# Expert weights of a mixture-of-experts layer in 2 MB blocks instead of 1 MB blocks

## The chip, the cores and the metric

The kernel runs on one core of one Trainium2 chip. The metric is the device time of one execution in microseconds (us). Three runs of the kernel before took 1173.51, 1174.28 and 1174.98 us, so their median is 1174.28 us. One further execution was taken by the profiler; all rows below come from it.

## The reference

One decoder layer on 256 tokens of width 1024, all in float32. Two attention branches work on one input projection, are gated, added and projected, and a layer norm gives `h`. Then 32 experts follow, of which each token uses four:

```
logits = h @ w_router + b_router
top_vals, top_idx = top_k(logits, 4);  gates = softmax(top_vals)
for each expert e:
    a   = h @ w_up[e] + b_up[e]                 # 1024 x 2048
    g   = min(a[:, :1024], 7);  lin = clip(a[:, 1024:], -7, 7)
    y   = ((lin + 1) * g * sigmoid(1.702 * g)) @ w_down[e] + b_down[e]   # 1024 x 1024
    acc = acc + combine[:, e] * y
out = layer_norm(2**0.25 * h + acc)
```

The weights of one expert are 8 MB (`w_up`) and 4 MB (`w_down`); all 32 are 384 MB (a MB of weights is 1,048,576 bytes here, and GB/s are decimal), and every one is read once from HBM.

## The kernel before, in words

**Stages.** First come projections and attention, with packed weights `w_pre` of 1 MB a block. Then the output stage (line 641 on) builds the two branches' mix and its projection, in eight steps `j`. Each step splits weight blocks into a high and a low part with `part`, on ScalarE and VectorE, into one of three scratch tiles: `sh`, `sy` and `sacc`. `sacc` lies in the place that the tile `acc` has later. Then the router chooses experts, and the expert stage works on pairs of experts `ea`, `ea + 1`: `gather` multiplies `h` by a selection matrix `pm` so that each expert's tokens (at most 64) stand in columns, `up_products` runs over eight row blocks `k` of `w_up`, `swiglu` and `transpose_y` follow, `down_products` runs over four blocks `a` of `w_down`, and `add_scattered` adds the pair's rows to `acc`. The last two pairs (28 and 30) are written out by hand: up of both, then down of both.

**Weight blocks.** `up_view` and `down_view` cut an expert into blocks of 128 partitions by 2048 numbers: 1 MB, 8 KB in each partition, contiguous in HBM. They land in tiles of the pools `ring1` (7), `ring2` (5), `ring3` (4), `ring4` (2) and `ringx` (2). `ring1` and `ring2` also carry the last `w_pre` blocks: a ring tile is free for an expert block as soon as its own `w_pre` block has been split. Twenty expert blocks (`ahead`) and two more, which land in `acc` and in `moe`'s tile `wy`, can be fetched before the first product.

**What sets the order.** All loads are issued by SyncE (SP, one queue). PE, VectorE and ScalarE follow the written order in the expert stage (`manual_schedule`); the order on SP is set by the framework's planner for the whole program. SP works strictly in order: a load that waits holds back every load behind it. Each load waits until its place is free, and eight completion semaphores are used in turn, so that a load also waits for the landing of the load eight places earlier.

The names that matter below: `acc`, `ahead`, `slot` (before) and `slot2` (after), `fetch_up`, `fetch_down`, `bias_parts` (line 564: loads `b_up` and `b_down` rows into the one tile `braw`, which GpSimd then works on), `columns`, and the hand-written last pairs.

Of the kernel before, what the change touches and what calls it, by code (L numbers as in the profile page):

```python
# [10 lines left out]
F32 = mybir.dt.float32  # L11
# [19 lines left out]
NR1, NR2, NR3, NR4, NRX, NSP = 7, 5, 4, 2, 2, 3  # L31
# [26 lines left out]
def decoder_layer(ctx: ExitStack, tc: tile.TileContext, A, dbg=None):  # L58
# [4 lines left out]
    ring1 = ctx.enter_context(tc.tile_pool(name="ring1", bufs=NR1))  # L63
# [15 lines left out]
    def slot(dtype=F32):  # L79

        if once:
            return once.pop()
        turn[0] += 1
        pool = seq[(turn[0] - 1) % len(seq)]
        return pool.tile([P, 2048], dtype, name="w", tag="x" if pool.name == "ringx" else "w")
# [457 lines left out]
    ring2 = ctx.enter_context(tc.tile_pool(name="ring2", bufs=NR2, reuse_waits="tile", side="right"))  # L543
    ringx = ctx.enter_context(tc.tile_pool(name="ringx", bufs=NRX, reuse_waits="tile", side="right"))
# [13 lines left out]
    ve.tensor_scalar(brd, ident[:NE, :NE], br, None, op0=OP.mult)  # L558
    wr = per.tile([P, KD, NE], F32, name="wr")
# [76 lines left out]
    ring4 = ctx.enter_context(tc.tile_pool(name="ring4", bufs=NR4, reuse_waits="tile", side="right"))  # L636
# [4 lines left out]
    for j in range(KD):  # L641
        if j % 2 == 0:
            wo = load(15 + 3 * (j // 2), 2)
        ps = misc().rearrange("p (a t) -> p a t", a=2)
        w = part(wo, j % 2, KD)
        for a, o in enumerate((oa, ob)):
            for k in range(4):
                mm3(ps[:, a], (w[0][:, 4 * a + k], w[1][:, 4 * a + k]), (o[0][:, k], o[1][:, k]),
                    k == 0, k == 3)
        t = held["g", j][1]  # L650
        ve.tensor_mul(t, ps, t)
        ve.tensor_add(t[:, 0], t[:, 0], t[:, 1])
        if j:
            w = part(wu, (j - 1) % 2, 1)
            for b in range(NT):
                w_out(j - 1, b, w)
        if j % 2 == 0:
            wu = load(27 + j // 2, 2)
        if j == 3:
            xr = ringx.tile([P, NT, D], F32, name="xr", tag="x")  # L660
# [11 lines left out]
    ring3 = ctx.enter_context(tc.tile_pool(name="ring3", bufs=NR3, reuse_waits="tile"))  # L672
# [90 lines left out]
    def shift_scale(dst, src, k, act):  # L763

        if act:
            se.activation(dst, src, AF.Identity, bias=lnT[:, 8 + k:9 + k], scale=lnT[:, k:k + 1])
        else:
            ve.tensor_scalar(dst, src, lnT[:, k:k + 1], lnT[:, 8 + k:9 + k], op0=OP.mult, op1=OP.add)  # L768
# [134 lines left out]
    def transpose_y(y, q, room):  # L903

        aT = y[:, 1].rearrange("p (j s) -> p j s", j=8)
        yv = y[:, 0].rearrange("s (a p i) -> s a i p", a=4, i=2)
        pt = room.rearrange("p (j s) -> p j s", j=4)
        for j in range(4):
            jj = 4 * q + j
            te.transpose(pt[:, j], yv[:, jj // 2, jj % 2, :], ident)  # L910
# [92 lines left out]
    with order:  # L1003
# [18 lines left out]
        for ea in range(0, NE - 4, 2):  # L1022
            for k in range(KD):
                if ea == 0 and k == 2:
                    xg[1] = gathered(gather(pm, 1), 1, lambda k4: k4 % 2 == 0)
                up_products(up, [fetch(fetch_up, ea + i, k) for i in range(2)], k)
# [21 lines left out]
            for a in range(4):  # L1048
                down_products(dn, aT, [fetch(fetch_down, ea + i, a) for i in range(2)], a)
# [15 lines left out]
        kept = seq[turn[0] % len(seq):] + seq[:turn[0] % len(seq)]  # L1065
        seq[:], turn[0] = [p for p in kept if p is not ringx], 0
        gb2, yb = [ringx.tile([P, 2048], F32, name="w", tag="x") for _ in range(2)]
        gb2, yb = gb2.rearrange("p (v n) -> p v n", v=4), yb.rearrange("p (a n) -> p a n", a=2)
        wup = {(e, k): fetch_up(e, k, slot()) for p in (ea, eb) for k in range(KD) for e in (p, p + 1)}
        wdn = {(e, a): fetch_down(e, a, slot()) for p in (ea, eb) for a in range(4) for e in (p, p + 1) if (p, a) != (eb, 3)}  # L1070
        for e in (eb, eb + 1):
            wdn[e, 3] = slot()
        for c, js in ((0, slice(0, 2)), (1, slice(0, 1)), (1, slice(1, 2))):
            for e in (eb, eb + 1):
                sy.dma_start(wdn[e, 3].rearrange("p (j f) -> p j f", j=2)[:, js, half(c)],
                             down_view(e)[:, 3, :].rearrange("p (j f) -> p j f", j=2)[:, js, half(c)])
        yp = slot(F32R).rearrange("p (a n) -> p a n", a=2)
        ups = lambda p, k: [wup[p + i, k] for i in range(2)]
        downs = lambda p, a: [wdn[p + i, a] for i in range(2)]
# [64 lines left out]
        down_products(dn, aTb, downs(eb, 3), 3, (0,))  # L1144
        parts(yp, dn, gs, 0)
# [38 lines left out]
    def more(e, base):  # L1184
# [15 lines left out]
        for kk in range(KD // 4):  # L1200
# [46 lines left out]
    w_up_rows = A["w_up"].rearrange("e (k p) f -> (e k) p f", p=P)  # L1247
    w_dn_rows = A["w_down"].rearrange("e (a p i) f -> (e a) p (i f)", p=P, i=2)
# [8 lines left out]
    with tc.If(most > 1):  # L1257
        at = slot().rearrange("p (v n) -> p v n", v=4)
# [67 lines left out]
def _layout(inputs):  # L1326
# [7 lines left out]
    arrays["norms"] = np.stack([arrays.pop(n) for n in ("ln1_g", "ln1_b", "ln2_g", "ln2_b")]).reshape(32, P)  # L1334
    arrays["w_pre"] = _pack(inputs)
# [26 lines left out]
```

## Time and profile before

| | |
|---|---|
| median of three runs | 1174.28 us |
| the profiled execution's own time | 1175.07 us |
| its span, first to last instruction | 1173.4 us |
| TensorE clock granted, mean | 0.996 |
| PE busy | 93% of the span |
| DMA queue that carries the loads, share of the 16 engines' span | 91.5% |
| DMA rate over the span, and in most slices from the tenth on | 375 GB/s, about 420 GB/s |

The profile divides the span into 40 slices of 29.3 us. Busy shares of several engines can be near 100% at once; which one ends the waits is read from the chain of waits, and for one stage from the chain in that stage. PE's busy time is modelled from pipelined matmuls, so that a busy PE is not a PE at its peak.

### The profile page before, as it was taken

Reading aid. Unit: us, or ns where it says so; the run is one execution under the profiler, and the core shown is the slowest. Engines: PE = TensorE matmul, PEld = TensorE weight load, DVE = VectorE, ACT = ScalarE, POOL = GpSimd, SP = SyncE. Lnnn points to the kernel's source line nnn. Section 1 sums busy time; section 2 is a strip of 40 time slices with the busy share of each in tenths; the row PEclk is TensorE's granted clock in tenths of the full one; section 3 lists DMA queues with packets and bytes.
Section 4 is the critical chain, followed back from the end, with each engine's and each line's share of the span. In section 5 each row is a group of like instructions: output and inputs, shape, how many; then the busy total and the mean of one; then the engine's idle time right before and its main releaser. Section 6 shows DMA issues by size and latency. Waiting matters only on the chain.

```text
span 1173.4 us, 14184 instructions
## 1 busy us (share of the span) xinstructions
PE 1092.3 (93%) x5807; PEld 576.1 (49%) x5808; DVE 331.7 (28%) x698; ACT 221.9 (19%) x427; POOL 136.7 (12%) x127
## 2 busy tenths in 40 slices
PE   7999999999999999999999999999999989899985
PEld 7888889744343343434444444343444444344332
DVE  7888636713122111111111111111111111111013
ACT  4557734321011010101010101010101010101011
POOL 5574563200000100000001000000000000000001
PEclk9999999999999999999999999999999999999998
DMA  8433659799999999999999999999999999999993
GB/s 325 182 109 144 240 201 381 294 409 388 421 420 421 419 405 420 420 421 419 421 420 420 420 420 421 419 421 420 420 421 420 420 419 421 421 420 421 421 419 145
DMA packets 64672, 439.74 MB, mean 375 GB/s; under 512 B 8486, under 2 KB 8731, under 8 KB 12251
## 3 DMA queue, kind: packets, MB, share of 16 engines
q1 hardware_dynamic: 64602, 438.79, 91.5%
q8 instruction: 47, 0.77, 0.3%
q14 instruction: 23, 0.18, 0.0%
HBM read 437.71 MB, written 1.05 MB: 374 GB/s over the span
## 4 chain that ended last, share of the span: by engine, by line
DMA 67%; PE 16%; DVE 1%; ACT 1%; issue 0%; SPq 0%; DVEq 0%; ACTq 0%
DMA w<-w_up 44%; DMA w<-w_down 23%; PE pair L1009 5%; PE bank L1016 2%; PE pair L1016 1%; PE misc L776 1%; PE misc L154 1%; PE misc L153 1%; PE misc L152 1%; PE pair L152 1%; PE pair L154 1%; PE pair L153 1%; PE bank L154 1%; PE bank L152 0%; PE bank L153 0%; PE misc L974 0%
## 5 line engine op out<-in xcount | busy, mean ns | idle before, releaser
L1009 PE MATMUL pair<-w,xg 128*64 128x512 f32 x2032 | 490.8, 597 | 43.3 <-DMA w<-w_up 43.3
L1009 PEld LDWEIGHTS pair<-w,xg 128*64 128x64 f32 x2032 | 178.7, 136 | 315.0 <-issue 195.2
L1016 PE MATMUL bank<-w,y 128*64 128x512 f32 x960 | 216.1, 596 | 3.8 <-DMA w<-w_down 2.1
L1016 PEld LDWEIGHTS bank<-w,y 128*64 128x64 f32 x960 | 71.2, 137 | 129.8 <-issue 111.9
L889 DVE TENSOR_TENSOR acc<-acc,misc 128x512 f32<-128x512 f32 x56 | 36.2, 684 | 163.3 <-PE misc L974 163.2
L152 PE MATMUL bank<-xh,wh 128*128 128x256 f32 x256 | 73.4, 287 | 4.3 <-DVE rm L205 2.5
L154 PE MATMUL bank<-xh,wl 128*128 128x256 f32 x256 | 72.5, 284 | 3.7 <-DVE wl L144 3.7
L153 PE MATMUL bank<-xl,wh 128*128 128x256 f32 x256 | 71.6, 280 | 1.4 <-DVE xl L149 1.4
L986 ACT CAST pgT<-bank 128x256 fp32r<-128x256 f32 x16 | 6.0, 373 | 351.2 <-PE bank L984 351.2
L899 DVE TENSOR_SCALAR y<-pair 128x512 f32<-128x512 f32 x30 | 20.6, 688 | 180.6 <-ACT y L892 180.6
L776 PEld LDWEIGHTS misc<-pm,h 128*128 128x128 f32 x512 | 59.8, 192 | 14.2 <-issue 11.7
L178 POOL TENSOR_TENSOR rstd<-rstd,mhalf 128x1 f32<-128x1 f32 x4 | 2.3, 571 | 545.4 <-DVE rstd L684 545.4
L962 DVE SCALAR_TENSOR_TENSOR yp<-bank,gsl,yp 128x512 fp32r<-128x512 f32 x30 | 21.1, 746 | 155.1 <-ACT yp L961 155.1
L776 PE MATMUL misc<-pm,h 128*128 128x128 f32 x512 | 64.2, 279 | 0.7 <-ACT y L911 0.7
L961 ACT ACTIVATE yp<-bank,gsl 128x512 fp32r<-128x512 f32 x30 | 19.0, 684 | 175.2 <-PE bank L1016 175.2
L152 PEld LDWEIGHTS bank<-xh,wh 128*128 128x128 f32 x256 | 48.0, 188 | 6.7 <-issue 3.1
L143 ACT CAST wh<-w 128x1024 fp32r<-128x1024 f32 (+1 forms) x42 | 42.7, 1023 | 41.7 <-PE bank L153 25.1
L892 ACT ACTIVATE y<-pair 128x512 f32<-128x512 f32 x30 | 17.8, 597 | 173.0 <-PE pair L1009 173.0
L154 PEld LDWEIGHTS bank<-xh,wl 128*128 128x128 f32 x256 | 48.0, 188 | 5.0 <-DVE wl L144 4.8
L153 PEld LDWEIGHTS bank<-xl,wh 128*128 128x128 f32 x256 | 48.1, 188 | 1.6 <-DVE xl L149 1.6
L768 DVE TENSOR_SCALAR xg<-misc,lnT 128x128 f32<-128x128 f32 x64 | 22.1, 405 | 88.4 <-PE misc L776 81.6
L144 DVE TENSOR_TENSOR wl<-w,wh 128x1024 fp32r<-128x1024 f32 (+1 forms) x26 | 41.6, 1604 | 15.4 <-ACT wh L143 15.4
(365 smaller groups left out, 1050.2 us busy)
## 6 DMA issues: line engine op xcount, KB each, us to landing
w<-w_up SPq DMA_DIRECT2D x254, 1024.0 KB, 19.9
w<-w_down SPq DMA_DIRECT2D x126, 1024.0 KB, 19.9
w<-w_pre SPq DMA_DIRECT2D x27, 1024.0 KB, 5.0
w<-w_pre SPq DMA_DIRECT2D x3, 512.0 KB, 7.2
w<-w_pre SPq DMA_DIRECT2D x2, 768.0 KB, 12.6
w<-xT SPq DMA_DIRECT2D x4, 256.0 KB, 6.3
xr<-x SPq DMA_DIRECT2D x2, 512.0 KB, 4.5
acc<-w_up SPq DMA_DIRECT2D x1, 1024.0 KB, 6.9
```

The source lines that it names most:

```text
L143: se.copy(hi, w[:, a])
L144: (ge if flip[0] in aside else ve).tensor_sub(lo, w[:, a], hi.bitcast(F32))
L152: te.matmul(out, lhs[0], rhs[0], start=start, stop=False)
L153: te.matmul(out, lhs[0], rhs[1], start=False, stop=False)
L154: te.matmul(out, lhs[1], rhs[0], start=False, stop=stop)
L768: ve.tensor_scalar(dst, src, lnT[:, k:k + 1], lnT[:, 8 + k:9 + k], op0=OP.mult, op1=OP.add)
L776: te.matmul(pt[:, k4], h[:, b, k * P:(k + 1) * P], pm[:, b].rearrange("p e s -> p (e s)"), start=(b == 0), stop=(b == NT - 1))
L889: ve.tensor_add(acc[:, b, half(c)], acc[:, b, half(c)], ps)
L899: ve.tensor_scalar(li, up[c][:, 1], LIMIT + 1.0, 1.0 - LIMIT, op0=OP.min, op1=OP.max)
L962: ve.scalar_tensor_tensor(y[:, 1, half(c)], dn[c], gs, y[:, 0, half(c)].bitcast(F32), op0=OP.mult, op1=OP.subtract)
L1009: te.matmul(up[c % 2][64 * i:64 * i + 64, c // 2], xg[k // 4][:, k % 4, 64 * i:64 * i + 64], ws[i][:, 512 * c:512 * c + 512], start=False, ...
L1016: te.matmul(dn[c][64 * i:64 * i + 64, :], aT[:, 2 * a + j, 64 * i:64 * i + 64], ws[i][:, D * j + 512 * c:D * j + 512 * c + 512], start=Fal ...
```

## The change

Blocks of the expert weights are 2 MB: `up_view` takes 256 rows of `w_up`, two neighbouring rows (16 KB) in each partition, and `down_view` 512 rows of `w_down`, four neighbouring rows (16 KB) in each partition. One load brings what two loads brought; `halves_of` gives the two halves to the products, which are as many and as large as before. Since a partition now holds rows 2p and 2p + 1 of `w_up`, `gather` takes every second column of `h` (`columns`), `transpose_y` every fourth column instead of every second, and the layer norm's scales for the gathered columns come from an extra small input, `ln1_up`, in that order.

The buffers are allocated anew. `ring1`, `ring2` and the tile of `x` (`xrows`) are released in front of the expert stage, and nine tiles of 2 MB are laid over their place and over the places of the earlier stages (`ring3` 5, `ringx` 3, `ring4` 1), with two tiles of 1 MB (`one1`, `one2`). With `acc` and `wy` that is 22 MB, as before.

```diff
-NR1, NR2, NR3, NR4, NRX, NSP = 7, 5, 4, 2, 2, 3
+NR1, NR2, NSP = 7, 5, 3
+NL2, NX2 = 5, 3
...
+    def slot2():
+
+        turn[0] += 1
+        return seq[(turn[0] - 1) % len(seq)].tile([P, 4096], F32, name="w2")
...
+    lnx = per.tile([P, 16], F32, name="lnx")
+    sy.dma_start(lnx, A["ln1_up"])
...
+    def columns(b, k):
+
+        return h[:, b].rearrange("p (k q i) -> p k i q", k=4, i=2)[:, k // 2, k % 2]
...
-                te.matmul(pt[:, k4], h[:, b, k * P:(k + 1) * P], pm[:, b].rearrange("p e s -> p (e s)"),
+                te.matmul(pt[:, k4], columns(b, k), pm[:, b].rearrange("p e s -> p (e s)"),
...
-    seq[:] = [ring4] * NR4 + order + [ringx] + [ring3] * NR3 + [ringx]
+
+    ring1.release()
+    xrows.release()
+    ring2.release()
+    ring3 = ctx.enter_context(tc.tile_pool(name="ring3", bufs=NL2, reuse_waits="tile"))
+    one1 = ctx.enter_context(tc.tile_pool(name="one1", bufs=1, reuse_waits="tile"))
+    ringx = ctx.enter_context(tc.tile_pool(name="ringx", bufs=NX2, reuse_waits="tile", side="right"))
+    one2 = ctx.enter_context(tc.tile_pool(name="one2", bufs=1, reuse_waits="tile", side="right"))
+    ring4 = ctx.enter_context(tc.tile_pool(name="ring4", bufs=1, reuse_waits="tile", side="right"))
+    rings((ring4, 1), (ring3, 3), (ringx, NX2), (ring3, NL2 - 3))
...
-        yv = y[:, 0].rearrange("s (a p i) -> s a i p", a=4, i=2)
+        yv = y[:, 0].rearrange("s (a p i) -> s a i p", a=2, i=4)
...
-        return A["w_up"][e].rearrange("(k p) f -> p k f", p=P)
+        return A["w_up"][e].rearrange("(k p i) f -> p k (i f)", p=P, i=2)
...
-        return A["w_down"][e].rearrange("(a p i) f -> p a (i f)", p=P, i=2)
+        return A["w_down"][e].rearrange("(a p i) f -> p a (i f)", p=P, i=4)
...
+    def halves_of(t):
+        return t[:, :2048], t[:, 2048:]
...
-    ahead = [(fetch_up, i, k) for k in range(KD) for i in range(2)][:-2]
-    ahead += [(fetch_down, i, a) for a in range(4) for i in range(2)][:NR1 + NR2 + NR3 + NR4 + NRX - len(ahead)]
-    early = {(f, e, k): f(e, k, slot()) for f, e, k in ahead}
-    early[fetch_up, 0, KD - 1] = fetch_up(0, KD - 1, acc.rearrange("p b d -> p (b d)"))
-    early[fetch_up, 1, KD - 1] = fetch_up(1, KD - 1, moe.tile([P, 2048], F32, name="wy", tag="y"))
+    ahead = [(fetch_up, i, k) for k in range(KD // 2) for i in range(2)][:-2]
+    ahead += [(fetch_down, i, a) for a in range(2) for i in range(2)][:NL2 + NX2 + 1 - len(ahead)]
+    early = {(f, e, k): f(e, k, slot2()) for f, e, k in ahead}
+    late = [[one2.tile([P, 2048], F32, name="w"), acc.rearrange("p b d -> p (b d)")],
+            [one1.tile([P, 2048], F32, name="w"), moe.tile([P, 2048], F32, name="wy", tag="y")]]
+    for i in range(2):
+        for t, src in zip(late[i], halves_of(up_view(i)[:, KD // 2 - 1])):
+            sy.dma_start(t, src)
+        early[fetch_up, i, KD // 2 - 1] = late[i]
...
+        wup = {(e, k): fetch_up(e, k, slot2()) for p in (ea, eb) for k in range(KD // 2) for e in (p, p + 1)}
+        wdn = {(e, a): fetch_down(e, a, slot2()) for p, a in ((ea, 0), (ea, 1), (eb, 0)) for e in (p, p + 1)}
         for e in (eb, eb + 1):
-            wdn[e, 3] = slot()
+            wdn[e, 1] = halves_of(slot2())
+            sy.dma_start(wdn[e, 1][0], halves_of(down_view(e)[:, 1])[0])
```

PE, VectorE, ScalarE and GpSimd have the same instructions in the same order but for a few neighbours that change places. SP's order is another one. Before, from the last `w_pre` blocks to the load into `wy` (`w<-w_up` and `w<-w_down` are expert blocks of 1 MB, `braw` are bias rows):

```order
L124 DMA w<-w_pre 128x2048 x2
L942 DMA w<-w_up 128x2048 x7
L567 DMA braw<-b_up 32x512 x3
L942 DMA w<-w_up 128x2048 x6
L567 DMA braw<-b_up 32x512 x3
L942 DMA w<-w_up 128x2048
L942 DMA acc<-w_up 128x2048
L946 DMA w<-w_down 128x2048 x5
L942 DMA wy<-w_up 128x2048
```

The same place after (128x4096 are blocks of 2 MB; `w_2703` is in `ring4`, `w_2705` the first in `ring3`, and the single `w<-w_up` behind `w_2719` goes to `one1`):

```order
L130 DMA w<-w_pre 128x2048 x2
L961 DMA w_2703<-w_up 128x4096
L575 DMA braw<-b_up 32x512 x6
L976 DMA acc<-w_up 128x2048
L961 DMA w_2705<-w_up 128x4096
L961 DMA w_2707<-w_up 128x4096
L961 DMA w_2709<-w_up 128x4096
L965 DMA w_2717<-w_down 128x4096
L965 DMA w_2719<-w_down 128x4096
L976 DMA w<-w_up 128x2048
L961 DMA w_2711<-w_up 128x4096
L961 DMA w_2713<-w_up 128x4096
```

Thirteen blocks of 1 MB stood ahead of the load into `acc`; now one block of 2 MB does. In both kernels one more block of 1 MB is issued earlier, right behind the loads of `x`. Second, SP at the end of the program, before:

```order
L942 DMA w<-w_up 128x2048 x32
L946 DMA w<-w_down 128x2048 x14
L1075 DMA w<-w_down 128x2x512 x2
L1075 DMA w<-w_down 128x512 x4
L1175 DMA out<-w 128x512 x4
```

and after (from the last four whole blocks of `w_down` on; `w_5892` and `w_5894` are the first halves of the last pair's `w_down`, `w_5896` and `w_5898` the second halves, in four loads each):

```order
L965 DMA w_5888<-w_down 128x4096
L965 DMA w_5890<-w_down 128x4096
L965 DMA w_5892<-w_down 128x4096
L965 DMA w_5894<-w_down 128x4096
L1098 DMA w_5896<-w_down 128x2048
L1103 DMA w_5896<-w_down 128x2x512
L1103 DMA w_5896<-w_down 128x512 x2
L1098 DMA w_5898<-w_down 128x2048
L1103 DMA w_5898<-w_down 128x2x512
L1103 DMA w_5898<-w_down 128x512 x2
```

Before, block `a = 0` of the last pair is complete with 6 MB still to come; after, with 4 MB still to come, and the two experts' last 2 MB stand one behind the other instead of in turns.

## Rows read from the trace of the kernel before

**Rows 1.** The page: GB/s in 40 slices, and the DMA packets.
```profile
GB/s 325 182 109 144 240 201 381 294 409 388 421 420 421 419 405 420 420 421 419 421 420 420 420 420 421 419 421 420 420 421 420 420 419 421 421 420 421 421 419 145
DMA packets 64672, 439.74 MB, mean 375 GB/s; under 512 B 8486, under 2 KB 8731, under 8 KB 12251
```

**Rows 2.** The page: the chain that ended last, shares by engine.
```profile
DMA 67%; PE 16%; DVE 1%; ACT 1%; issue 0%; SPq 0%; DVEq 0%; ACTq 0%
```

**Rows 3.** SP's own waits: who was waited for, total us, times, longest.
```profile
SPq L942 <- DMA w<-w_up: 238.9, 114, 3.4
```

**Rows 4.** Stretches: engines' busy us (instructions), PEclk, DMA share, GB/s.
```profile
1000.00:1100.00 100.00, 93.48 (x455) 41.98 (x456) 15.49 (x32) 11.70 (x24) 0.00 (x0) 1.00 1.01 420
1150.00:1155.00 5.00, 5.00 (x26) 1.72 (x24) 0.00 (x0) 0.00 (x0) 0.00 (x0) 1.00 0.50 188
1154.00:1155.00 1.00, 1.00 (x8) 0.35 (x6) 0.00 (x0) 0.00 (x0) 0.00 (x0) 1.00 0.26 98
1155.00:1160.00 5.00, 4.31 (x19) 1.58 (x15) 2.10 (x4) 1.38 (x2) 0.00 (x0) 1.00 0.00 0
```

**Rows 5.** SP's queue in time, 136 to 222 us: start, us, load, count.
```profile
136.95 0.42 SPq L946 DMA_DIRECT2D w<-w_down  x1
...
172.80 11.68 SPq L942 DMA_DIRECT2D w<-w_up  x7
...
189.90 25.61 SPq L942 DMA_DIRECT2D w<-w_up  x6
...
220.76 0.35 SPq L942 DMA_DIRECT2D w<-w_up  x1
221.21 0.37 SPq L942 DMA_DIRECT2D acc<-w_up  x1
```

**Rows 6.** PE in time: the last product that reads `sacc`.
```profile
220.90 0.28 PE L154 MATMUL misc<-bh,sacc 128*128 128x256 f32 x1
```

**Rows 7.** Stretches around the start of the expert stage, columns as in rows 4.
```profile
200.00:221.20 21.20, 21.20 (x139) 19.36 (x138) 15.81 (x18) 8.99 (x11) 7.92 (x7) 1.00 0.62 226
225.00:230.00 5.00, 4.46 (x40) 3.17 (x38) 4.46 (x9) 1.66 (x4) 0.25 (x1) 1.00 1.02 431
280.00:290.00 10.00, 10.00 (x49) 3.36 (x48) 2.11 (x4) 0.00 (x0) 0.00 (x0) 1.00 0.81 326
```

**Rows 8.** The chain in time at the program's end: start, us, what.
```profile
1120.20 19.85 DMA w<-w_down
...
1140.10 3.65 PE pair L1016 x14
...
1147.50 10.45 PE pair L1016 x48
1157.95 0.68 PE misc L974 x2
```

**Rows 9.** The chain in time, first two pairs of experts: start, us, what.
```profile
237.37 7.02 PE pair L1009 x32
...
246.37 10.45 PE pair L1009 x48
...
280.16 10.45 PE bank L1016 x48
...
291.47 6.87 PE pair L1009 x32
...
344.13 3.46 PE pair L1009 x16
```

**Rows 10.** PE's waits: who was waited for, total us, times, longest.
```profile
PE pair L1009 <- DMA w<-w_up: 43.3, 39, 2.5
```

**Rows 11.** The last stretch, columns as in rows 4.
```profile
1165.00:1174.00 9.00, 0.00 (x0) 0.00 (x0) 2.67 (x4) 1.17 (x2) 2.18 (x2) 0.50 0.33 120
```

**Rows 12.** Weight loads by line: ns min/median/max, first and last start, form.
```profile
L910 PEld LDWEIGHTS misc<-ident,y x120: 194/209/219, 270.8 to 1089.1; 128*128 128x128 f32 x120
...
L721 PEld LDWEIGHTS bank<-ident,h x16: 138/141/143, 226.3 to 229.4; 128*128 128x128 f32 x16
```

More of the change, by code (lines that the diff above doesn't have):

```diff
@@ L84, in slot @@
         pool = seq[(turn[0] - 1) % len(seq)]
-        return pool.tile([P, 2048], dtype, name="w", tag="x" if pool.name == "ringx" else "w")
+        return pool.tile([P, 2048], dtype, name="w")
+    def slot2():
+        turn[0] += 1
+        return seq[(turn[0] - 1) % len(seq)].tile([P, 4096], F32, name="w2")
     def rings(*pools):
@@ L542, in decoder_layer @@
     moe = ctx.enter_context(tc.tile_pool(name="moe", bufs=1, reuse_waits="tile", side="right"))
-    ring2 = ctx.enter_context(tc.tile_pool(name="ring2", bufs=NR2, reuse_waits="tile", side="right"))
-    ringx = ctx.enter_context(tc.tile_pool(name="ringx", bufs=NRX, reuse_waits="tile", side="right"))
+    ring2 = tc.alloc_tile_pool(name="ring2", bufs=NR2, reuse_waits="tile", side="right")
+    xrows = tc.alloc_tile_pool(name="xrows", bufs=1, reuse_waits="tile", side="right")
     rings((ring1, NR1), (ring2, NR2))
@@ L635, in decoder_layer @@
     src.release()
-    ring4 = ctx.enter_context(tc.tile_pool(name="ring4", bufs=NR4, reuse_waits="tile", side="right"))
     wg, rt, lnT = router_tables()
@@ L659, in decoder_layer @@
         if j == 3:
-            xr = ringx.tile([P, NT, D], F32, name="xr", tag="x")
+            xr = xrows.tile([P, NT, D], F32, name="xr")
             for b in range(NT):
@@ L671, in decoder_layer @@
     pre.release()
-    ring3 = ctx.enter_context(tc.tile_pool(name="ring3", bufs=NR3, reuse_waits="tile"))
     def bn(src, b, c):
@@ L765, in shift_scale @@
         if act:
-            se.activation(dst, src, AF.Identity, bias=lnT[:, 8 + k:9 + k], scale=lnT[:, k:k + 1])
+            se.activation(dst, src, AF.Identity, bias=lnx[:, 8 + k:9 + k], scale=lnx[:, k:k + 1])
         else:
-            ve.tensor_scalar(dst, src, lnT[:, k:k + 1], lnT[:, 8 + k:9 + k], op0=OP.mult, op1=OP.add)
+            ve.tensor_scalar(dst, src, lnx[:, k:k + 1], lnx[:, 8 + k:9 + k], op0=OP.mult, op1=OP.add)
+    def columns(b, k):
+        return h[:, b].rearrange("p (k q i) -> p k i q", k=4, i=2)[:, k // 2, k % 2]
     def gather(pm, kk, some=(0, 4)):
@@ L1025, in decoder_layer @@
                     xg[1] = gathered(gather(pm, 1), 1, lambda k4: k4 % 2 == 0)
-                up_products(up, [fetch(fetch_up, ea + i, k) for i in range(2)], k)
+                if k % 2 == 0:
+                    ws = [fetch(fetch_up, ea + i, k // 2) for i in range(2)]
+                up_products(up, [w[k % 2] for w in ws], k)
                 if ea == 0 and k == 4:
@@ L1048, in decoder_layer @@
             for a in range(4):
-                down_products(dn, aT, [fetch(fetch_down, ea + i, a) for i in range(2)], a)
+                if a % 2 == 0:
+                    ws = [fetch(fetch_down, ea + i, a // 2) for i in range(2)]
+                down_products(dn, aT, [w[a % 2] for w in ws], a)
                 if a == 0:
@@ L1064, in decoder_layer @@
         ea, eb = NE - 4, NE - 2
[L1065 to L1070, printed above, removed]
+        gb2 = one1.tile([P, 2048], F32, name="w").rearrange("p (v n) -> p v n", v=4)
+        yb = one2.tile([P, 2048], F32, name="w").rearrange("p (a n) -> p a n", a=2)
+        wup = {(e, k): fetch_up(e, k, slot2()) for p in (ea, eb) for k in range(KD // 2) for e in (p, p + 1)}
+        wdn = {(e, a): fetch_down(e, a, slot2()) for p, a in ((ea, 0), (ea, 1), (eb, 0)) for e in (p, p + 1)}
         for e in (eb, eb + 1):
-            wdn[e, 3] = slot()
+            wdn[e, 1] = halves_of(slot2())
+            sy.dma_start(wdn[e, 1][0], halves_of(down_view(e)[:, 1])[0])
         for c, js in ((0, slice(0, 2)), (1, slice(0, 1)), (1, slice(1, 2))):
             for e in (eb, eb + 1):
[L1075 to L1079, printed above, removed]
+                to, of = [t.rearrange("p (j f) -> p j f", j=2)[:, js, half(c)] for t in
+                          (wdn[e, 1][1], halves_of(down_view(e)[:, 1])[1])]
+                sy.dma_start(to, of)
+        ups = lambda p, k: [wup[p + i, k // 2][k % 2] for i in range(2)]
+        downs = lambda p, a: [wdn[p + i, a // 2][a % 2] for i in range(2)]
         for k in range(KD):
@@ L1144, in decoder_layer @@
         down_products(dn, aTb, downs(eb, 3), 3, (0,))
+        yp = moe.tile([P, 2, FF], F32R, name="yp", tag="y")
         parts(yp, dn, gs, 0)
@@ L1159, in final @@
         gb = lambda i, c: at[:, 2 * i + c]
-        rows = slot().rearrange("p (b d) -> p b d", b=NT)
+        rows = slot2()[:, :2048].rearrange("p (b d) -> p b d", b=NT)
         dst = lambda b, c: rows[:, b, half(c)]
@@ L1188, in more @@
         ve.tensor_copy(gt, gate[:, :, ds(e, 1)].rearrange("p b o -> p (b o)"))
-        bu = slot()[0:1, :]
+        bu = slot2()[0:1, :2048]
         sy.dma_start(bu, A["b_up"][ds(e, 1), :])
-        bd = slot()[0:1, :D]
+        bd = slot2()[0:1, :D]
         sy.dma_start(bd, A["b_down"][ds(e, 1), :])
@@ L1206, in more @@
                 for b in range(NT):
-                    te.matmul(pt[:, k4], h[:, b, k * P:(k + 1) * P], pm[:, b], start=(b == 0), stop=(b == NT - 1))
+                    te.matmul(pt[:, k4], columns(b, k), pm[:, b], start=(b == 0), stop=(b == NT - 1))
             for k4 in range(4):
@@ L1218, in more @@
         for k in range(KD):
-            t = slot()
-            sy.dma_start(t, w_up_rows[ds(e * KD + k, 1)].rearrange("a p f -> p (a f)"))
+            if k % 2 == 0:
+                t2 = slot2()
+                sy.dma_start(t2, w_up_rows[ds(e * (KD // 2) + k // 2, 1)].rearrange("a p f -> p (a f)"))
+            t = halves_of(t2)[k % 2]
             for c in range(4):
@@ L1232, in more @@
         for a in range(4):
-            t = slot()
-            sy.dma_start(t, w_dn_rows[ds(e * 4 + a, 1)].rearrange("a p f -> p (a f)"))
+            if a % 2 == 0:
+                t2 = slot2()
+                sy.dma_start(t2, w_dn_rows[ds(e * 2 + a // 2, 1)].rearrange("a p f -> p (a f)"))
+            t = halves_of(t2)[a % 2]
             for j in range(2):
@@ L1245, in more @@
                 add_rows(b, c, pa)
-    w_up_rows = A["w_up"].rearrange("e (k p) f -> (e k) p f", p=P)
-    w_dn_rows = A["w_down"].rearrange("e (a p i) f -> (e a) p (i f)", p=P, i=2)
+    w_up_rows = A["w_up"].rearrange("e (k p i) f -> (e k) p (i f)", p=P, i=2)
+    w_dn_rows = A["w_down"].rearrange("e (a p i) f -> (e a) p (i f)", p=P, i=4)
     most = nc.values_load(nblk_i[0:1, NE:NE + 1], min_val=0, max_val=T // CAP)
@@ L1334, in _layout @@
     arrays["norms"] = np.stack([arrays.pop(n) for n in ("ln1_g", "ln1_b", "ln2_g", "ln2_b")]).reshape(32, P)
+    ln1 = np.stack([np.asarray(inputs[n]).reshape(KD // 2, P, 2) for n in ("ln1_g", "ln1_b")])
+    arrays["ln1_up"] = np.ascontiguousarray(ln1.transpose(2, 0, 1, 3)).reshape(P, 16)
     arrays["w_pre"] = _pack(inputs)
```

15 lines of the change are left out of this document (6 added, 9 removed).

## Prediction

> **What bounds the kernel now.** I read the page first. From the tenth slice to the last but one the loads run at about 420 GB/s [rows 1], and the chain that ended last is 67% DMA [rows 2]: past the first few slices the time is the time of a stream of weights. Next, is that stream starved? In the stretch from 1000 to 1100 us the 16 DMA engines are busy all the time (share 1.01, 420 GB/s) [rows 4], while SP mostly waits for the landing of an earlier load [rows 3]: loads are always queued, so neither issuing nor latency is in the way. One MB then takes 1.0486 MB / 420 GB/s = 2.50 us. Two things can move the end: the rate of the stream, and how much of the 384 MB has landed before it starts to run without a gap. The third is the tail behind the last landing. The last load traffic is seen in 1154 to 1155 us and none after [rows 4], so the stream ends at 1155.
>
> **The change part by part.**
>
> *The stock before the stream.* Before, SP issues a block as soon as one ring tile is free: between 172.80 and 215.5 us thirteen blocks, and one at 136.95 [rows 5]. So 14 MB are there or on their way when the unbroken stream begins, with the load at 220.76. Afterwards (order of SP) only one block of 2 MB and the early 1 MB stand ahead of the load into `acc`. That load overwrites `sacc`, and PE's last product that reads `sacc` starts at 220.90 and takes 0.28 [rows 6]: this is why `acc` was issued at 221.21 [rows 5], and nothing before that product changes on PE. Behind it in SP's queue wait four blocks of 2 MB of the next pools' places and everything else, though parts of these places are free from 184 us on (by the thirteen issues). So 3 MB instead of 14 are there: 11 MB x 2.50 = 27.5 us more of stream, and a start 221.21 - 220.76 = 0.45 later. The six loads of bias rows ahead of `acc` wait for GpSimd, but they hold the queue only while it is held anyway. That DMA idles from about 203 to 223 us is the visible form of this; before, 200 to 221 already had only 226 GB/s [rows 7].
>
> *Given back.* Before, the stream stops once more, because the stock is full and PE has not freed a tile: 280 to 290 us has a share of 0.81 instead of 1.01, which is 2.0 us [rows 7]. Afterwards there is no stock to be full: -2.0.
>
> *The rate.* The trace has no packet of 16 KB from these queues, so I work out the cost of a packet from two sizes. From 1000 to 1100 us nearly all packets are of 8 KB (384 MB in rows of 8 KB are 49152 of the 64672 packets [rows 1]): 16 engines x 1.01 / 420 GB/s = 38.5 ps a byte, 315 ns a packet. From 1150 to 1155 only the last pieces, in rows of 2 KB, move: 16 x 0.50 / 188 = 42.6 ps a byte, 87 ns a packet [rows 4]. The line through both has 37.1 ps a byte and 11 ns a packet, by the last digit of the shares 10 to 12.5. A packet of 16 KB then takes 11 + 608 = 619 ns instead of 2 x 315: -1.8%, or -1.6% with 10 ns. Bounds: no gain (the rows are cut to 8 KB on the way, or a byte costs what it costs): 0; all of the 11 ns in 315 gone: -3.5%. A loss through other addresses in HBM I see no row for. I take -1.7%, for 374 of the 381 MB that remain (the rest are blocks of 1 MB): 374 x 2.50 x 1.7% = -15.9 us. Range of this term: 0 to -32.7.
>
> [...]
>
> *The tail.* PE's last stretch starts when block `a = 0` of the last pair is complete, at 1140.10, 14.9 us or 6 MB before the end of the stream, and is unbroken PE work from there until 1157.95, 17.85 us; the rest takes 1173.4 - 1157.95 = 15.45 [rows 8]. Afterwards that block comes with its neighbour, 4 MB before the end: 4 x 2.50 x 0.983 = 9.8 us. PE's 17.85 us are the same, so the end lies 5.1 us further behind the last landing: +5.1. The turned order of the last 2 MB is within this, since PE reaches those blocks only later.
>
> *What costs nothing.* PE's work for one pair is 344.13 - 291.47 = 52.7 us [rows 9], a pair's 24 MB take 24 x 2.50 x 0.983 = 58.9 us: 6.2 us of cover a pair. Under it lie the strided weight loads: the transposes that read every second column load in 209 ns, those with neighbouring columns in 138 to 141 [rows 12]; 32 loads of a pair's gathers at +70 ns are 2.2 us, with both ends 0 and (twice as long) about 4. The extra load `lnx` is 0.4 us on SP while SP has time. Fewer, larger buffers: 18 MB in nine tiles hold eight loads in flight and the pair in use, so that the stream isn't throttled.
>
> *Sum.* +27.5 + 0.45 - 2.0 - 15.9 + 5.1 = +15.1. Span 1173.4 + 15.1 = 1188.5, the profiled execution's own time 1175.07 + 15.1 = 1190.2. The median of the runs is 0.8 under that execution: 1189.4, I say 1189.
>
> **The rivals.**
>
> *No gain in rate.* The same sum without the 15.9: 1205. For it: at 420 GB/s and a share of 1.01 the engines are full, and what a packet costs beside its bytes rests on a 5 us stretch in which half of the engines are already done.
>
> *Slower still through PE.* In the first pair PE comes to block `k = 4` at 246.37 + 2/3 x 10.45 = 253.3 [rows 9]. If `acc` lands at 226, the second block that holds `k = 4` (`w_2713`) is the seventh of 2 MB behind it in SP's order, with one of 1 MB among them: 226 + 7 x 4.91 + 2.5 = 262.9. So PE waits 9.6 us, against 2.5 at the longest before [rows 10]. [...] PE is late by 9 us in the first pair; a stall of the stream follows only if the block in `ringx`'s third tile is freed after about 297 (the loads issued until then end at 300), and `down` of `a = 1` frees it at 280.16 + 3.5 + 9 = 293. [...]
>
> *The other side: the queue isn't held.* If the blocks in `ring3` could go at the times at which their places fell free before (184 to 215 us), the 27.5 and 0.45 would go, the full stock's 2.0 would stay, and the sum be -10.9: 1163. It decides at the half: the kernel is faster if more than 6 of the 11 MB have landed by 221, that is if the second block of 2 MB is issued before about 205. Against it stands SP's order itself, which has `acc` ahead, and the product at 220.90.
>
> *The rate rises further.* To undo the loss of 31 us (the sum without its rate term) the stream must be 3.3% faster: 434 GB/s sustained. For it: single stretches have 431 [rows 7]. Against: it would take nearly all of what a packet costs. It gives 1174, no change, and at -3.5% 1173. [...]
>
> **How the numbers follow.** Chances: forecast 0.70, no gain 0.13, PE 0.09, rate much higher 0.05, queue not held 0.03. The forecast's own range (gain 1.2 to 2.3%) is 1183 to 1194; for 8 in 10 I take in most of PE's case and of the no-gain case, and gains up to 2.6%: 1180 to 1203. 0.2% (2.3 us) is what the measurement can tell from no change: faster by more is the queue's case and a third of the high rates, 0.05; within it 0.03; slower 0.92.
>
> **What would show it.** In the profile of the changed kernel: SP issues one 2 MB block near 182, then bias rows, then `acc` near 221 and five blocks of 2 MB behind it; the DMA share is near 0 from 203 to 222. The stream from 300 on shows 426 to 428 GB/s, and the page about 37,700 packets (24,064 fewer of weights, and some 3000 small ones that go with 188 fewer loads). PE waits 8 to 11 us for `w_up` near 253. The last PE stretch starts 10 us before the last landing, the landing lies near 1165. A rate of 420 proves the rate term wrong, an issue of several 2 MB blocks before 215 the first term; a span under 1178 proves the whole wrong.

## The result and the profile after

The changed kernel takes 1191.11 us (median of 4 runs, 1189.80 to 1193.14), the kernel before 1174.45 beside it (4 runs, 1173.51 to 1174.98): ratio 1.0144, 95% interval 1.0126 to 1.0162. Its profiled execution took 1190.18 us with a span of 1188.5, so 15.1 us more span than before (the prediction had 1189 for the median, 1180 to 1203, and +15.1 for the span).

First SP's queue in time (start, us, load, count), which answers to [rows 5]:

```profile
180.99 0.33 SPq L961 DMA_DIRECT2D w<-w_up  x1
181.49 18.31 SPq L575 DMA_DIRECT2D braw<-b_up  x6
220.38 0.35 SPq L976 DMA_DIRECT2D acc<-w_up  x1
220.77 2.73 SPq L961 DMA_DIRECT2D w<-w_up  x3
```

One block of 2 MB, six loads of bias rows, and then nothing until `acc` at 220.38. Before, thirteen blocks of 1 MB went out between 172.80 and 215.5 [rows 5]. The stretches (engines' busy us and instructions, PEclk, DMA share, GB/s) answer to [rows 4, 7]:

```profile
200.00:221.20 21.20, 21.20 (x139) 19.31 (x139) 15.79 (x22) 8.88 (x11) 1.99 (x1) 1.00 0.02 6
225.00:300.00 75.00, 62.97 (x351) 28.27 (x351) 20.65 (x66) 14.48 (x27) 2.02 (x6) 0.93 1.01 427
280.00:290.00 10.00, 9.21 (x60) 5.90 (x60) 3.87 (x6) 3.57 (x8) 0.00 (x0) 1.00 1.01 430
...
1000.00:1100.00 100.00, 94.71 (x454) 38.49 (x452) 18.45 (x38) 11.11 (x23) 0.00 (x0) 1.00 1.01 427
...
1164.00:1166.00 2.00, 2.00 (x12) 0.72 (x10) 0.00 (x0) 0.00 (x0) 0.00 (x0) 1.00 0.02 9
1166.00:1170.00 4.00, 4.00 (x20) 1.29 (x18) 0.00 (x0) 0.00 (x0) 0.00 (x0) 1.00 0.00 0
```

DMA rests from 200 to 221 (6 GB/s, before 226), then runs without a gap at 427 GB/s, also in 280 to 290, where the kernel before stood still for 2 us. The stream ends at 1165, ten us after that of before (the last packets of weights end at 1164.8 and 1154.8). The page (its GB/s slices and packets, as in [rows 1]) has the rest:

```profile
GB/s 323 178 108 142 264 189 84 228 426 427 427 427 428 426 416 427 428 426 429 425 429 426 427 428 427 426 427 427 427 428 426 428 426 427 428 426 428 427 410 69
DMA packets 37740, 439.71 MB, mean 370 GB/s; under 512 B 5621, under 2 KB 5866, under 8 KB 9386
```

The chain in time at the end, as in [rows 8]:

```profile
1122.41 32.55 DMA w<-w_down
...
1155.01 3.65 PE pair L1039 x14
...
1162.41 10.45 PE pair L1039 x48
1172.87 0.68 PE misc L997 x2
```

PE's last stretch starts at the landing near 1155, ten us before the last one; before it was fifteen. From the last landing to the end of the span it is 23.7 us, before 18.6. So two thirds of the loss lie in the stream (1155 to 1165), one third behind it.

### The profile page after: what moved, and what is told of

It is laid out like the page before. It is cut to its first block, busy times and chain, and to the rows that moved or that the text cites. A ratio compares the mean times of both kernels' runs of the same rounds, so it can differ in the third digit from the quotient of the medians.

```text
span 1188.5 us, 13798 instructions
## 1 busy us (share of the span) xinstructions
PE 1109.3 (93%) x5807; PEld 554.2 (47%) x5808; DVE 332.6 (28%) x698; ACT 221.7 (19%) x427; POOL 135.9 (11%) x127
## 2 busy tenths in 40 slices
DMA packets 37740, 439.71 MB, mean 370 GB/s; under 512 B 5621, under 2 KB 5866, under 8 KB 9386
## 4 chain that ended last, share of the span: by engine, by line
DMA 43%; PE 41%; DVE 2%; ACT 1%; issue 0%; SPq 0%; DVEq 0%; ACTq 0%
DMA w<-w_up 37%; PE bank L1039 15%; PE pair L1032 13%; DMA w<-w_down 5%; PE misc L786 4%; PE misc L926 1%; PE pair L1039 1%; ACT y L927 1%; PE misc L158 1%; PE misc L160 1%; PE misc L159 1%; PE pair L159 1%; PE pair L160 1%; PE pair L158 1%; PE misc L997 1%; DMA braw<-b_down 0%
## 5 line engine op out<-in xcount | busy, mean ns | idle before, releaser
L1032 PE MATMUL pair<-w,xg 128*64 128x512 f32 x2032 | 501.1, 599 | 41.8 <-DMA w<-w_up 41.8
L1032 PEld LDWEIGHTS pair<-w,xg 128*64 128x64 f32 x2032 | 150.3, 137 | 352.0 <-issue 272.0
L1039 PE MATMUL bank<-w,y 128*64 128x512 f32 x960 | 218.7, 596 | 5.1 <-DMA w<-w_down 3.4
L906 DVE TENSOR_TENSOR acc<-acc,misc 128x512 f32<-128x512 f32 x56 | 36.2, 684 | 173.5 <-PE misc L997 173.3
L786 PEld LDWEIGHTS misc<-pm,h 128*128 128x128 f32 x512 | 62.9, 197 | 14.2 <-issue 11.7
L786 PE MATMUL misc<-pm,h 128*128 128x128 f32 x512 | 67.4, 285 | 0.7 <-ACT y L927 0.7
L774 DVE TENSOR_SCALAR xg<-misc,lnx 128x128 f32<-128x128 f32 x64 | 22.1, 404 | 92.5 <-PE misc L786 85.5
L581 POOL CAST bup<-braw 96x512 bf16<-96x512 f32 x4 | 2.4, 607 | 375.5 <-PE pair L800 375.4
```

The source lines that it names most:

```text
L774: ve.tensor_scalar(dst, src, lnx[:, k:k + 1], lnx[:, 8 + k:9 + k], op0=OP.mult, op1=OP.add)
L786: te.matmul(pt[:, k4], columns(b, k), pm[:, b].rearrange("p e s -> p (e s)"), start=(b == 0), stop=(b == NT - 1))
L906: ve.tensor_add(acc[:, b, half(c)], acc[:, b, half(c)], ps)
L1032: te.matmul(up[c % 2][64 * i:64 * i + 64, c // 2], xg[k // 4][:, k % 4, 64 * i:64 * i + 64], ws[i][:, 512 * c:512 * c + 512], start=False, ...
L1039: te.matmul(dn[c][64 * i:64 * i + 64, :], aT[:, 2 * a + j, 64 * i:64 * i + 64], ws[i][:, D * j + 512 * c:D * j + 512 * c + 512], start=Fal ...
```

## Experiments

The theory is the sum of the prediction. To weigh it I also summed the trace's packets of 2 KB and more and took what is still to come (MB of 1.0486 million bytes, as in the prediction):

| kernel | at 221 us | at 300 us | us per MB, 300 to 1100 |
|---|---|---|---|
| before | 371.9 | 342.0 | 2.498 |
| changed | 382.8 | 351.3 | 2.457 |
| e1_places | 376.2 | 346.1 | 2.459 |
| e2_rows8 | 382.8 | 351.5 | 2.495 |
| e6_held | 383.9 | 356.3 | 2.471 |
| e8_written | 371.9 | 341.8 | 2.471 |
| e10_gap_before | 371.9 | 342.4 | 2.471 |

**The stock, given back: e1_places.**

```
-    ring3 = ctx.enter_context(tc.tile_pool(name="ring3", bufs=NL2, reuse_waits="tile"))
+    low = [ctx.enter_context(tc.tile_pool(name=f"low{i}", bufs=1, reuse_waits="tile")) for i in range(NL2)]
...
-    ringx = ctx.enter_context(tc.tile_pool(name="ringx", bufs=NX2, reuse_waits="tile", side="right"))
+    top = [ctx.enter_context(tc.tile_pool(name=f"top{i}", bufs=1, reuse_waits="tile", side="right")) for i in range(NX2)]
...
-    rings((ring4, 1), (ring3, 3), (ringx, NX2), (ring3, NL2 - 3))
+    rings(*((p, 1) for p in (top[1], ring4, low[1], low[2], low[0], top[0], low[3], low[4], top[2])))
```

> The changed kernel with one pool for each place of 2 MB instead of two ring pools, the places handed out in about the order in which the work before leaves them. Sizes, packets and the end of the kernel are those of the changed kernel. By the prediction's first term (weights that are not yet there when the unbroken stream begins): two 2 MB blocks go out at once after the bias rows, near 200, and three more near 212, so that the unbroken stream begins near 212 with 6 MB there instead of near 221 with 3 MB. That is 3 MB and 9 us of stream, 6.6 MB in all at 2.46 us, 16 us: 1175 us (1171 to 1178), no slower than the kernel before. Rival 1, the loss is PE's wait of 9 to 10 us in the first pair and the halved clock behind it: at most those 10 us come back, 1181 or more. Rival 2, the loss is the coarse size of the buffers, each freed as a whole: nothing comes back, 1190 to 1192.

Measured: 1176.87 us (11 runs), ratio to before 1.0022 (1.0013 to 1.0031), so 14.2 us under the changed kernel. SP's queue, and two stretches:

```profile
181.67 0.33 SPq L961 DMA_DIRECT2D w<-w_up  x1
182.17 18.16 SPq L575 DMA_DIRECT2D braw<-b_up  x6
200.43 20.51 SPq L961 DMA_DIRECT2D w<-w_up  x5
221.06 0.36 SPq L976 DMA_DIRECT2D acc<-w_up  x1
```

```profile
200.00:221.20 21.20, 21.20 (x139) 19.30 (x139) 15.69 (x22) 8.97 (x11) 1.94 (x1) 1.00 0.93 356
...
280.00:290.00 10.00, 10.00 (x50) 3.45 (x50) 2.22 (x4) 0.00 (x0) 0.00 (x0) 1.00 0.58 209
```

Five blocks go out between 200 and 221 although sizes, packets and PE's work are those of the changed kernel. Both rivals fall: more than PE's 10 us came back, and the coarse blocks are still there. Coarse blocks do have a price, but another one: with the places full the stream stands still for 4 of the 10 us from 280 on, where the kernel before stood for 2.

**The stock, taken away from the kernel before: e6_held.**

```
+    late = per.tile([P, 1], F32, name="late")
+    ge.tensor_copy(late, h[:, 0, :1])
+    for n, (f, e, k) in enumerate(ahead):
+        t = slot()
+        if n > 1:
+            ge.tensor_copy(t[:, :1], late)
+        early[f, e, k] = f(e, k, t)
...
```

> The kernel before with its 1 MB loads of 8 KB rows, but all expert loads from the third on wait for one column that GpSimd writes into their buffers when the residual is there: the queue of weights is held, and nothing else of the change is made. 18 copies of one column on GpSimd are added. By the prediction's first term: the unbroken stream begins near 233 with 3 to 4 MB there, where the kernel before has some 17 MB by then; 13 to 14 MB at 2.50 us, less the 2 us that its stream stands still while the buffers are full: 31 to 34 us, 1207 us (1200 to 1214). Rival, the loss of the change comes from its larger blocks or its end, and loads held back are made up behind PE: 1174 to 1181.

Measured: 1202.02 us (1.0233, 1.0217 to 1.0248). The queue was held as meant:

```profile
182.87 17.46 SPq L567 DMA_DIRECT2D braw<-b_up  x6
221.32 0.35 SPq L942 DMA_DIRECT2D acc<-w_up  x1
231.89 0.35 SPq L942 DMA_DIRECT2D wy<-w_up  x1
233.39 15.86 SPq L942 DMA_DIRECT2D w<-w_up  x12
```

```profile
300.00:400.00 100.00, 96.13 (x476) 43.23 (x474) 18.17 (x37) 9.56 (x20) 0.00 (x0) 1.00 1.01 425
```

With 1 MB loads in rows of 8 KB and the old end of the program the kernel is 28 us slower, so the stock alone can cost more than the whole change did. But 5 us of the expected time are missing, and the stream ran at 425 GB/s where the same packets had 420 before. That was not in any theory; e8 to e13 follow it up.

**The rows: e2_rows8.**

```
-        return A["w_up"][e].rearrange("(k p i) f -> p k (i f)", p=P, i=2)
+        return A["w_up"][e].rearrange("(k i p) f -> p k i f", p=P, i=2)
...
-        return A["w_down"][e].rearrange("(a p i) f -> p a (i f)", p=P, i=4)
+        return A["w_down"][e].rearrange("(a b p i) f -> p a b (i f)", b=2, p=P, i=2)
...
```

> The changed kernel with its 2 MB loads, buffers, places and order, but each partition takes two rows of 8 KB that lie 1 MB apart instead of one of 16 KB; the gathers take adjacent columns again. By the prediction's third term (a fixed cost of about 11 ns in each packet): some 24,000 packets more, about 61,800 in all, the stream back at 420 GB/s instead of 427, 374 MB at 2.50 instead of 2.457 us per MB, so 16 us more than the changed kernel: 1207 us (1203 to 1211). Rival, the rate came from half as many loads, twice as large, and not from the rows: 427 GB/s stay, 1190 to 1193.

Measured: 1206.19 us (1.0270, 1.0254 to 1.0286), 15.1 us over the changed kernel.

```profile
DMA packets 61804, 439.71 MB, mean 365 GB/s; under 512 B 5621, under 2 KB 5866, under 8 KB 9386
```

```profile
300.00:400.00 100.00, 99.75 (x514) 40.63 (x512) 20.04 (x40) 10.83 (x22) 0.00 (x0) 1.00 1.01 420
1000.00:1100.00 100.00, 92.87 (x430) 35.99 (x428) 14.63 (x30) 9.19 (x18) 0.00 (x0) 1.00 1.01 421
```

Loads of 2 MB in rows of 8 KB have the old rate. Larger loads bring nothing here, longer rows do. Not all of the 15.1 us is rate, though. In e2's profile the last weights land at 1178.6, 13.8 us after those of the changed kernel; 1.6 us lie behind it: PE's wait for `w_down` ended at 1168.81, and the granted clock was 0.50 from 1170 to 1172. A stretch, and PE's products after the wait in the chain:

```profile
1170.00:1172.00 2.00, 2.00 (x6) 0.48 (x4) 0.00 (x0) 0.00 (x0) 0.00 (x0) 0.50 0.88 335
...
1168.81 5.22 PE pair L1039 x14
```

The same fourteen products took 3.65 us in the changed kernel, from 1155.01 on, at a granted clock of 1.00.

**The tail: e4_tail and e7_tail_halves.** e4 loads the last pair's blocks by halves, e7 also the second block of the pair before; e7's edit:

```
-        wdn = {(e, a): fetch_down(e, a, slot2()) for p, a in ((ea, 0), (ea, 1), (eb, 0)) for e in (p, p + 1)}
-        for e in (eb, eb + 1):
-            wdn[e, 1] = halves_of(slot2())
-            sy.dma_start(wdn[e, 1][0], halves_of(down_view(e)[:, 1])[0])
+        wdn = {(e, 0): fetch_down(e, 0, slot2()) for e in (ea, ea + 1)}
+        for p, a in ((ea, 1), (eb, 0), (eb, 1)):
+            for e in (p, p + 1):
+                wdn[e, a] = halves_of(slot2())
+            for i in range(1 if (p, a) == (eb, 1) else 2):
+                for e in (p, p + 1):
+                    sy.dma_start(wdn[e, a][i], halves_of(down_view(e)[:, a])[i])
```

> The changed kernel, in which the last pair's w_down blocks are loaded by halves of 1 MB, both experts in turn, so that the rows of the first products are complete 6 MB before the end instead of 4. By the prediction's fourth term, PE's last unbroken stretch starts 5 us earlier against the last landing, and 5 us come back: 1186 us (1184 to 1188). Rival, the end hangs on the last landing and the slowest DMA engine alone: 1190 to 1192.

> The changed kernel, in which the last pair's w_down blocks are loaded by halves in turn for both experts, from the first expert pair's second block on: e4_tail did so for the very last pair alone, gave back 1.9 us, and there PE came to the last pair's products from a block of the pair before, which landed at 1146.0, with 6.9 us of its own products still to do. Theory, the tail is a chain of landings and each whole 2 MB block in it holds PE: with both blocks halved the last pair's first products start with their landing near 1151.1, 18.7 us before the end of PE's work, 2.3 us earlier than in e4_tail, so 1187 us (1186 to 1188), 4 us under the changed kernel. Rival, what is left after e4_tail is the time of the last landing: 1189 to 1190.

Measured: 1189.24 us (1.0126, 1.0110 to 1.0141) and 1189.50 us (1.0129, 1.0113 to 1.0145): 1.9 and 1.6 us back, not 5 and 4. In e4 PE came to the last pair's products at 1153.4 from the whole 2 MB block of the pair before, which landed at 1146.08. In e7, which halves that block too, the chain before PE's last stretch is:

```profile
1129.15 23.49 DMA w<-w_down
1152.64 0.04 issue
1152.69 3.65 PE pair L1039 x14
```

PE still waits for a landing, 2.3 us earlier than in the changed kernel. The reason is in the program's order of loads: both halves of a place become free at once, and the scheduler put the two halves of expert 30 ahead of those of expert 31, not in turn. So PE's first product of the pair waits for 3 of the pair's 4 MB instead of all 4, and 1 MB at 2.46 us is what its start gained. The order that I meant has not been run; that the other half of the tail would come back with it is argued, not shown.

**Together, and one place more: e5_places_halves and e9_split.** e5 has the edits of e1 and e7. e9 adds a tenth place:

```
+        pool = seq[(turn[0] - 1) % len(seq)]
+        if pool is None:
+            return [p.tile([P, 2048], F32, name="w") for p in (one1, one2)]
...
+    seq.insert(6, None)
...
```

> The edits of e1_places and e7_tail_halves together. Theory: e1_places is a span of 1175.2 in which the last stretch of PE starts at a landing at 1141.65; halved blocks bring that start to 1138, so 3.6 us less: 1173.2 us (1172 to 1174.3), just under the kernel before or equal to it. Rival, PE is behind anyway in e1_places, whose last weights land 8 us before PE's last product of them ends: 1176 to 1178.

> e5_places_halves with one place of 2 MB more between the first and the last pair: the two single places of 1 MB that stand unused there are taken together as a tenth place, its blocks loaded as two of 1 MB with 8 KB rows. Theory: in e1_places the stream stands still for 3 to 4 us between 225 and 300 because all places are full; 2 MB more take that away, against 1 us for the share of 8 KB rows: 2.6 us under e5_places_halves, 1170.6 us (1168.5 to 1173). Rival, the weights not loaded there are not missed later, PE sets the end: equal to e5_places_halves.

Measured: e5 1174.38 us (1.0000, 0.9991 to 1.0009), 2.5 us under e1 and equal to before; e9 1171.11 us (0.9974, 0.9963 to 0.9985), 3.3 us under e5. The stretch from 280 on, in e9:

```profile
280.00:290.00 10.00, 10.00 (x54) 3.40 (x50) 0.96 (x2) 0.40 (x1) 0.00 (x0) 1.00 1.01 412
```

The share is 1.01 again: the stand still was a matter of places, and weights not loaded there were missed at the end.

**The 425 GB/s: e8_written, e10_gap_before, e11_gap_after, e12_gap_split, e13_off.** e8 is e6 with `late` copied from a table (`ident`) that is there from the start. e10, e11 and e12 add one line to the kernel before, the changed kernel and e9:

```
     acc = per.tile([P, NT, D], F32, name="acc")
+    per.tile([P, 1], F32, name="gap")
```

e13 instead adds `cst.tile([P, 8], F32, name="gap")` at the left edge of the kernel before.

> The kernel e6_held, but the 18 columns that GpSimd writes come from a table that is there from the start, so that no load waits for the residual. e6_held's stream ran at 425 GB/s, the kernel before at 420 with the same packets. Theory, the held queue made e6_held slower and its rate has nothing to do with the writes: 420 GB/s, 1175 us (1174 to 1178). Rival, the writes or the shifted order of the queue alone bring 425 GB/s: 1164 to 1169.

> The kernel before with one unused tile of 4 bytes per partition beside acc. It moves the places on the right side (9 of the 20 that the ring of 1 MB loads uses) down by 32 bytes, from an address that leaves 32 by division through 64 to one that leaves 0; order, loads and sizes stay. e8_written, which had such a tile too, was 8 us faster at 425 GB/s instead of 420. Theory, the address decides the packet's time: mean packet of 8 KB 310.7 ns instead of 314.4, 425 GB/s, 1166 us (1164 to 1168). Rival, GpSimd's writes in e8_written or its other order of bias loads did it: 1173 to 1176.

> The changed kernel with the same unused tile: its right side (4 of the 9 places of 2 MB) goes down by 32 bytes, to a multiple of 64 as the left side is. If the address costs by the byte: the 16 KB packet goes from 616.3 ns by 7.6 to 608.7, 1.2% of the stream from 221 to 1165 us, 11 us: 1180 us (1178 to 1182). If it costs by the packet: by 3.8 to 612.5, 0.6%, 5.5 us: 1185.5 (1184 to 1187). Rival, 16 KB rows don't feel it: 1190 to 1192.

> e9_split with the same unused tile. Theory by the byte: 11 us less than 1171: 1160 us (1158 to 1163); by the packet: 1165.6 (1164 to 1167). Either is under the kernel before. Rival, PE sets the end there: 1169 to 1172.

> The kernel before with an unused tile of 32 bytes per partition at the left edge: the left side, 11 of the 20 places, moves up by 32 bytes, so that now every place of the ring leaves 32 by division through 64. Theory: with 0 of 20 such places 425 GB/s, with 9 of 20 420; with 20 of 20 the packet takes 314.4 + 3.8 x 11/9 = 319 ns, 414 GB/s, 1.5% of the 930 us of stream, 14 us more: 1188 us (1183 to 1192). Rival, what counts is that both sides lie at the same offset: 425 GB/s, 1166. Second rival, the left side's address is nothing: 1174.

| run | us | ratio to before | mean packet, 600 to 900 us | right side's address in a partition (from the built program), over a multiple of 256 |
|---|---|---|---|---|
| before | 1174.1 | 1 | 314.4 ns (8 KB) | 32 |
| e8_written | 1165.87 | 0.9925 (0.9909 to 0.9940) | 310.6 ns (8 KB) | 0 |
| e10_gap_before | 1165.82 | 0.9931 (0.9917 to 0.9944) | 310.6 ns (8 KB) | 0 |
| e13_off | 1173.77 | 0.9998 (0.9989 to 1.0007) | 314.3 ns (8 KB) | 32 |
| changed | 1191.11 | 1.0144 (1.0126 to 1.0162) | 616.3 ns (16 KB) | 224 |
| e11_gap_after | 1191.01 | 1.0144 (1.0129 to 1.0160) | 616.0 ns (16 KB) | 192 |
| e12_gap_split | 1170.09 | 0.9969 (0.9957 to 0.9980) | 616.2 ns (16 KB) | 192 |

Stretches of e10, beside the 420 GB/s of [rows 4]:

```profile
300.00:400.00 100.00, 99.75 (x511) 40.60 (x512) 20.05 (x40) 10.81 (x22) 2.97 (x4) 1.00 1.01 425
1000.00:1100.00 100.00, 94.67 (x465) 43.20 (x462) 15.49 (x32) 11.68 (x24) 0.00 (x0) 1.00 1.01 425
```

and the same stretch of e13:

```profile
300.00:400.00 100.00, 99.75 (x510) 40.36 (x508) 19.10 (x39) 10.81 (x22) 4.12 (x5) 1.00 1.01 420
```

An unused tile of 4 bytes makes the kernel before 8 us faster. e8's theory fell, its rival (the edit brings the rate even when nothing is held) came true, and e10 shows that neither GpSimd's writes nor the order of loads is needed. e8 is also the right kernel to hold e6 against: the same tile at the same address, and only what `late` is copied from, and so the wait, differs. Held back, it takes 36.2 us more; at 300 us 14.5 MB more are still to come, at 2.471 us each 35.8. So holding cost 36 where 31 to 34 were expected, and the address gave back 8: this makes the 28 of e6.

My theory for e11 to e13, that a multiple of 64 is enough and every place counts alike, fell three times. So I laid the packets of 320 to 430 us beside the loads, in order of time, and these beside their places in the built program. In e10 the nine right places, at multiples of 4096, take 309.0 ns a packet nearly throughout; the left ones, 64 over a multiple of 256, take 309 in some loads and 313.5 in others. In the kernel before and in e13 every place is at 313 to 315, among them the left ones of before, at a multiple of 64; and e11 moved its right side from 32 over a multiple of 64 to 0 for nothing. So in these runs a multiple of 64 did not suffice (616.0 ns in e11 against 616.3), and one of 4096 did (309.0 ns in e10, 8 KB); they don't tell what holds for the multiples between.

The left loads of e10 at 309 ns stand directly behind right ones in time: of four left loads behind three right ones the first two, of seven behind six the first four. So what a load costs hangs not on its own place alone; why stays open.

e10, level with e8, is the fastest version that was run, under both kernels: 8.3 us under the one before, 25 under the changed one. The changed kernel's rows with places at such multiples were not tried: e11 and e12 moved them to an address that isn't one.

## Why the prediction was right

The median is 1191.11 against 1189, the profiled execution 1190.18 against 1190.2. The 2 us between the medians come from the last step of the sum: the prediction put the median 0.8 under the profiled execution, as in the kernel before, but here it lies 0.9 above.

*The stock.* Right, in place and size. The load into `acc` held the queue, and at 221 us 10.9 MB more were still to come than before; the prediction had 11. At 300 us it is 9.3 MB: the rest is the stop with full places, which fell away as said, and the higher rate in between. e1 moves the stock one way and e6 the other (against e8, with everything else kept), and the time follows both.

*The rate.* 427 GB/s and 37,740 packets, as foretold. e2 measures the term by itself: 13.8 us up to the last landing, against 15.9. The step behind it was only half right. I took 11 ns as a cost that every packet has. Two packets of 8 KB do take 629 - 616 = 13 ns longer than one of 16 KB, but e10 takes 2 x 3.8 ns off two packets of 8 KB without touching a row, by the address alone. In that the number was lucky: the kernel before, the changed one and e2 all lie off that address, and rows of 16 KB on it were not run.

*Stream and tail.* Stock, stop and rate together are 10.05 us in the prediction; the last landing moved by 10.0, from 1154.8 to 1164.8. The tail was to lose 5.1: from PE's last stretch to the last landing it is 10 us instead of 15, and from that landing to the end 23.7 instead of 18.6. That the size of a block in the last pair sets this is supported by the other runs: it is 18.5 to 18.7 us in e6, e8 and e10, which end with blocks of 1 MB, 23.7 in e1, which ends with 2 MB, and 21.7 in e4 and e7. The whole 5.1 was not undone by any run of the changed kernel.

*What was to cost nothing.* A pair's products take 52.8 us of PE in the changed kernel (303.40 to 356.16 in its chain), 52.7 before, so nothing was lost there. But the price of the strided gathers was read from the wrong lines: [rows 12] compares transposes of two different tiles. The gathers' own weight loads, with adjacent columns before and every second column after:

```profile
L776 PEld LDWEIGHTS misc<-pm,h x512: 186/192/202, 235.3 to 1084.1; 128*128 128x128 f32 x171
L786 PEld LDWEIGHTS misc<-pm,h x512: 193/196/208, 234.4 to 1097.3; 128*128 128x128 f32 x171
```

That is 4 ns a load, not 70.

*PE's wait.* It came where it was expected (who was waited for, total us, times, longest, from 225 to 300 us; compare [rows 10]), and in two parts:

```profile
PE pair L1032 <- DMA w<-w_up: 8.8, 2, 5.9
```

```profile
258.59 1.94 PE L1032 MATMUL pair<-w,xg 128*64 128x512 f32 x2 [5.88 <-DMA w<-w_up]
263.41 5.25 PE L1032 MATMUL pair<-w,xg 128*64 128x512 f32 x14 [2.88 <-DMA w<-w_up]
```

The granted clock fell too, to the 0.50 that the kernel before shows from 1165 on, behind PE's last work [rows 11]:

```profile
257.00:258.00 1.00, 0.00 (x0) 0.00 (x0) 0.00 (x0) 0.00 (x0) 0.00 (x0) 0.50 0.92 393
262.00:263.00 1.00, 0.00 (x0) 0.00 (x0) 0.00 (x0) 0.00 (x0) 0.00 (x0) 0.50 1.04 442
266.00:267.00 1.00, 1.00 (x6) 0.37 (x4) 0.00 (x0) 0.00 (x0) 0.00 (x0) 0.67 1.03 418
267.00:268.00 1.00, 1.00 (x5) 0.27 (x2) 0.00 (x0) 0.00 (x0) 0.00 (x0) 1.00 0.98 393
```

PE had run out of work near 253, was granted 0.50 at 257, and 1.00 again from 267, when it had been multiplying since 263.4. It cost nothing that the end shows: the stream ran at a share of 0.99 to 1.03 in every 10 us from 230 to 300, and PE made up for it under the 6 us of cover in each pair: from 270 on it waits for no load until 454.85.

*The other rivals.* No gain in rate: refuted by 427 GB/s and by e2, which is that rival built (1206 against its 1205, with 1.6 of the clock in it). A queue that isn't held: refuted by SP's rows; e1 shows what it is worth, though less than the rival's 1163, since at 221 us 4.3 MB more than before were still to come, and the coarse places fill earlier. A still higher rate did not come.

## What to carry to other kernels

Where a stream of weights sets the time, count the bytes that are still to come when it starts to run without a gap: one long wait at the head of an in-order queue held back 10.9 MB here, 27 us, more than the 14 to 15 that longer rows gave, and a pool for each place, handed out in the order in which they fall free, gave 14 back. After an edit that should reorder loads, read the order that the scheduler made of it: halves of one buffer that become free together stayed together, and most of the gain that I expected did not come. And try the address of a buffer before making rows longer: e10 gained 8.3 us by it.

## What was not expected of the hardware

A shift of nine of the twenty places by 32 bytes changes a packet of 8 KB from 314.4 to 310.6 ns in the mean, 420 to 425 GB/s, and the kernel by 0.7% (e10). Rows of 16 KB in loads of 2 MB have 427 GB/s, rows of 8 KB in loads of the same size 420 to 421 (e2) and in loads of 1 MB 420 (before): the length of the load made no difference here.
